# Expert weights of a two-layer hybrid encoder: two experts of a pair in one transfer, and the last down matrix in tiles

## The chip, the cores and the metric

The kernel runs on one core of a Trainium2 chip. The metric is the device time of one execution in microseconds, the median of three runs. A profiled execution of its own gives the trace; durations below come from that one.

## The reference, cut to what matters

Two layers (DEPTH 2), 256 tokens of width 1024, all in float32. A layer is a mixer (an mLSTM branch and an attention branch, merged, projected, added to x) and then a mixture of 32 experts. What the change touches is the second half:

```
t = rms_norm(x) * (1 + scale2) + shift2               # 256 x 1024
combine[256, 32] = weights of the top 2 experts of the top group, else 0
for 32 experts e:
    act = silu(t @ w_gate[e]) * (t @ w_up[e]) * combine[:, e]     # 1024 x 512 twice
    out += act @ w_down[e]                                        # 512 x 1024
x = x + gate2 * out
```

Each expert has three matrices of 2 MB, so a layer reads 192 MB of expert weights, once each. (MB and KB of tiles are binary here; the GB/s and MB of profile rows are decimal.)

## The kernel before, in words

**Places for weights.** A weight tile is 1 MB: 128 partitions times `SLOT` = 2048 floats (8 KB per partition). Tiles stand in numbered slots: 16 of one large buffer, the arena (`at`, L96), three of a region "y" and four of a region "x" (`region`, L83), one spare in the mixer. The mixer uses most of the arena for its own data and streams its weights through four arena slots (`BASE`: 0, 1, 2, 15), the three y slots and a few that are lent for a time. In the experts 18 slots take weights: 13 of the arena, three y, two x. They come free one after the other as the mixer ends: `release` at L1030 (8, 11, 12), in the order word `free:7:13:14` (L50), at L1073 (y and 6), at L1112 (x) and at L1400 (4 and 5).

**The order of transfers.** The whole list of weight tiles is written out beforehand (`plan`, L123, filled at L249 to L288): per pair of experts gate, up and down, each in two halves `h` of the contraction, each half as one tile of expert 2i and one of expert 2i+1, so 12 tiles a pair. `pump` (L162) takes the next entry, picks the first free slot that `fits` (L138) allows, and issues one transfer from SP's queue (L176); if no slot is free, the list waits. `done` (L185) gives a slot back after its last matmul and pumps again. All of this is decided when the program is built; on the chip SP runs the transfers in that order, each waiting for the readers of its slot.

**The experts.** 16 pairs (L1417). At most 64 rows of an expert are gathered (CAP), so the two experts of a pair share PE side by side, each in 64 of its 128 columns. `gate_up` (L1264) takes for each half both experts' tiles and interleaves their matmuls; then `act_mul`, `act_T`, and `down` (L1287), `leave`, `scatter`. Every other pair gathers rows for two pairs. After pair 11 (`MIDDLE`) comes `rest` (L1384): a conditional block for experts with more than 64 rows, with SP transfers of its own into tile `y` (L1367, L1377). The down matrix of the last pair is read by `down_last` (L1327) in two halves of 512 output columns; its transfers (L277 to L282) cut the columns out of a tile of 1024, so that each is 512 KB in pieces of 2 KB.

**Between layers.** The plan goes on with the next layer's first modulation tiles ("ada", `EARLY`), which `fits` lets into BASE, y, and arena slots 11 and 13 (L146), and with the mixer's weights.

**Queues.** Weights go by SP's queue alone. ACT's and POOL's queues carry a few small loads. PE and SP follow the program's order (`MANUAL`, L59).

Of the kernel before, what the change touches and what calls it, by code (L numbers as in the profile page):

```python
# [18 lines left out]
P = 128  # L19
# [4 lines left out]
DEPTH = 2  # L24
# [15 lines left out]
ONCE = (8, 9, 10, 11)  # L40
MIDDLE = 11
BF16 = mybir.dt.bfloat16
EARLY = (4, 5)
FIRST = (0, 2, 1, 3)
PREP = 60
# [14 lines left out]


def trunk(ctx, tc, x, c, b_ada, b_in, mlstm_norm_g, norm2_g, final_g,
          rope, gate_t, up_t, down_t, ada_t, in_t, branch_t, out_t, packs, router, out, dbg=None, depth=DEPTH):
    nc = tc.nc
    V, A, G, T = nc.vector, nc.scalar, nc.gpsimd, nc.tensor
    dbg = dbg or {}
# [12 lines left out]

    pools = {}  # L80
    tiles = {}

    def region(kind, name, types, side=None):  # L83

        if kind in pools:
            assert not any(r[1][0] == kind for r in ring.values())
            pools.pop(kind).close()
        es = ExitStack()
        pool = es.enter_context(tc.tile_pool(name=name, bufs=1, reuse_waits="tile", side=side))
        tiles[kind] = [pool.tile([P, SLOT], dt, name=f"{name}{i}") for i, dt in enumerate(types)]  # L90
        pools[kind] = es

    def wide(t, off, a):
# [2 lines left out]
    def at(slot, off, *shape):  # L96
        n = 1
        for s in shape:
            n *= s
        a = arena[:, slot * SLOT + off:slot * SLOT + off + n]  # L100
# [37 lines left out]
    def fits(slot, key):  # L138
        kind, s = slot
        if kind == "z":  # L140
            return key[0] not in ("wg", "wu", "wd", "fin")
        late = key[0] in ("wg", "wu", "wd", "wm", "wa", "wo")
        if (late and st["phase"] > 4 * key[1]) or slot in usual or (slot in opened and st["phase"] % 4 < 2):
            return True
        if key[0] == "ada" and kind == "a" and key[2] in ((EARLY, range(4))[key[1] == 0]):
            return s in (ONCE if key[1] == 0 else (11, 13))  # L146
        return False

    def release(slots):
# [12 lines left out]
    def pump():  # L162
        while st["sent"] < len(plan):
            key, src, shape, phase = plan[st["sent"]]
            if phase > st["phase"]:
                return
            if shape is None:
                src()
            else:
# [79 lines left out]
    for l in range(depth):  # L249
        if l == 0:  # L250
            for b in FIRST:
                plan_ada(0, b)
        else:
            plan_ada(l, EARLY[0])
        for it in stream(l):
            if it[0] in DENSE:
                sh = (8, 256) if it[0] == "akv" else (4, 512)
                add((it[0], l, *it[1:]), in_t[l, W_IN.index(it)].rearrange("p (k c) -> p k c", k=sh[0]), sh)
            elif it[0] == "r":
                plan_ada(l, it[1])  # L260
            else:
                plan_ada(l + 1, it[1])
            if l and it == ("q", 0, 0):
                plan_ada(l, EARLY[1])
            if it == ("k", 0, 0):
                add(("late", l), lambda l=l: late_loads(l), None, 4 * l)
            if it == ("k", 0, 1):
                add(("late2", l), lambda l=l: late_loads2(l), None, 4 * l)
        for j in range(2):
            for i, nm in enumerate(("wm", "wa")):  # L270
                add((nm, l, j), branch_t[l, i, j].rearrange("p (k c) -> p k c", k=4), (4, 512))
        for j in range(2):
# [26 lines left out]
    maskt = cst.tile([P, 3, P], F32, name="maskt")  # L299
    iot = cst.tile([P, P], F32, name="iot")  # L300
    desc = cst.tile([P, 8], F32, name="desc")
    fold = cst.tile([P, 32], F32, name="fold")
    fold2 = cst.tile([P, 64], F32, name="fold2")
    xs = cst.tile([P, NT, D], F32, name="xs")
# [12 lines left out]
    def setup():  # L317
# [140 lines left out]


    def mixer(l, p):  # L460
        region("x", f"R{l}", [F32R] * 4)
# [449 lines left out]

        def branch():
            if not yy:
                region("y", f"Y{l}", [F32R] * 3, "right")
# [157 lines left out]
        region("y", f"B{l}", [F32] * 3, "right")  # L1072
# [27 lines left out]
        region("x", f"X{l}", [F32] * 2 + [F32R] * 2)  # L1100
        return pL, lc, ssn, xa, sh2c


    def experts(l, p, pL, lc, ssn, xa, sh2c):
# [222 lines left out]
        def down_last(i, owT):  # L1327

            for n in range(2):
                pd = ps.tile([P, 512], F32, tag="f", name=f"pd{n}")  # L1330
                for h in range(2):
                    w = [wt("wd", l, 2 * i + e, n, h) for e in range(2)]
                    for kk in range(2):
                        for e in range(2):
                            T.matmul(pd[CAP * e:CAP * e + CAP, :], lhsT=aT[:, 2 * h + kk, CAP * e:CAP * e + CAP],  # L1335
                                     rhs=w[e][:, kk, :], start=h == 0 and kk == 0, stop=h == 1 and kk == 1,
                                     tile_position=(0, CAP * e))
                    for e in range(2):
                        done("wd", l, 2 * i + e, n, h)
# [7 lines left out]
                turn_rows(range(2, 4))  # L1347


        def rest_block(e, base):  # L1350
# [12 lines left out]
            for w in (gate_t, up_t):  # L1363
                pg = ps.tile([P, 512], F32, tag="f", name="pgr")
                for h in range(4):
                    wc = y.rearrange("p (a b) -> p a b", a=2)
                    nc.sync.dma_start(wc, w[l, ds(e, 1), h // 2].rearrange("o p (k f) -> p (o k) f", k=4)  # L1367
                                      [:, 2 * (h % 2):2 * (h % 2) + 2])
# [5 lines left out]
            act_T()  # L1374
            pd = [ps.tile([P, 512], F32, tag="f", name="pdr0"), ps.tile([P, 512], F32, tag="f", name="pdr1")]
            for k in range(4):
                nc.sync.dma_start(y, down_t[l, ds(e, 1), k // 2].rearrange("o p (k f) -> p (o k) f", k=2)[:, k % 2])  # L1377
# [6 lines left out]
        def rest():  # L1384
            full = nc.values_load(ci[0:1, NE:NE + 1], min_val=0, max_val=S,
                                  skip_runtime_bounds_check_because="a count of at most 256 rows")
            with tc.If(full > CAP):
                with tc.For_i(0, NE, 1) as e:
                    ne = nc.values_load(ci[0:1, ds(e, 1)], min_val=0, max_val=S,
                                        skip_runtime_bounds_check_because="a count of at most 256 rows")  # L1390
                    with tc.If(ne > CAP):
                        for base in (CAP, CAP + P):
                            rest_block(e, base)

        nextp = None
        oh = onehot(0)
# [61 lines left out]
    region("y", "B", [F32] * 3, "right")  # L1458
    with tc.manual_schedule(engines=MANUAL):
        p = setup()  # L1460
        for l in range(depth):
# [33 lines left out]
def laid_out(inputs):  # L1495
# [22 lines left out]
    def every(a):  # L1518
# [14 lines left out]
    return {**experts, "ada_t": whole(ada, (L, 12, 2, P, SLOT)), "in_t": whole(np.stack(tiles, 1), (L, len(W_IN), P, SLOT)),  # L1533
            "branch_t": whole(branch, (L, 2, 2, P, SLOT)), "out_t": whole(wo, (L, 2, 2, P, SLOT)),
            "packs": whole(packs, (L, P, NPK)), "router": whole(router, (L, P, 288))}

# [25 lines left out]
```

## Time and profile before

| | |
|---|---|
| median of 3 runs | 1473.15 us (1472.9 to 1474.9) |
| the profiled execution | 1472.51 us, of which the span (first to last instruction) is 1470.4 us |
| PE busy | 1336.9 us (91%); TensorE's granted clock 0.974 on average |
| DVE, ACT, POOL busy | 42%, 27%, 18% of the span |
| DMA | 521.31 MB in 77542 packets, 355 GB/s on average |
| weight tiles | SP's queue, 86.5% of 16 DMA engines' time over the span |

The page gives the busy time of each engine, and the span in 40 slices of 36.8 us. A busy PE is not a PE at its peak, since the ends of matmuls are modelled. A packet is one piece that one of the 16 DMA engines moves; the packets under 512 B are the marks of 4 bytes with which an engine reports its part of a transfer.

### The profile page before, as it was taken

Reading aid. Unit: us, or ns where it says so; the run is one execution under the profiler, and the core shown is the slowest. Engines: PE = TensorE matmul, PEld = TensorE weight load, DVE = VectorE, ACT = ScalarE, POOL = GpSimd, SP = SyncE. Lnnn points to the kernel's source line nnn. Section 1 sums busy time; section 2 is a strip of 40 time slices with the busy share of each in tenths; the row PEclk is TensorE's granted clock in tenths of the full one; section 3 lists DMA queues with packets and bytes.
Section 4 is the critical chain, followed back from the end, with each engine's and each line's share of the span. In section 5 each row is a group of like instructions: output and inputs, shape, how many; then the busy total and the mean of one; then the engine's idle time right before and its main releaser. Section 6 shows DMA issues by size and latency. Waiting matters only on the chain. (4 is left out here: it accounts for less than half of the span.)

```text
span 1470.4 us, 20138 instructions
## 1 busy us (share of the span) xinstructions
PE 1336.9 (91%) x7836; PEld 777.5 (53%) x7837; DVE 617.7 (42%) x1376; ACT 403.3 (27%) x755; POOL 263.5 (18%) x295
## 2 busy tenths in 40 slices
PE   6899998799999989889889999998999999987996
PEld 3778788734443434334359788883443443433432
DVE  3786755613323213213268777553332232223223
ACT  3636563311111101001056366541110110101101
POOL 2543336200000000000035533550000000000000
PEclk8999999899999999999999999998999999999998
DMA  9966697589999999999996645667999999999996
GB/s 383 368 257 238 253 366 276 205 367 419 419 420 419 420 420 419 420 393 399 413 411 258 241 175 233 233 261 294 420 419 419 420 419 419 420 419 418 372 420 236
DMA packets 77542, 521.31 MB, mean 355 GB/s; under 512 B 9472, under 2 KB 9472, under 8 KB 16256
## 3 DMA queue, kind: packets, MB, share of 16 engines
q1 hardware_dynamic: 75968, 515.95, 86.5%
q0 software_dynamic: 608, 2.14, 0.4%
q10 hardware_dynamic: 864, 1.85, 0.3%
q8 instruction: 65, 1.06, 0.3%
q14 instruction: 37, 0.30, 0.1%
HBM read 518.86 MB, written 1.05 MB: 354 GB/s over the span
## 5 line engine op out<-in xcount | busy, mean ns | idle before, releaser
L1270 PE MATMUL pgu<-arena 128*64 128x512 f32 x1504 | 376.0, 595 | 21.1 <-DMA arena<-in_up_t_dram 13.0
L1270 PEld LDWEIGHTS pgu<-arena 128*64 128x64 f32 x1504 | 121.6, 137 | 246.7 <-issue 193.7
L1279 DVE SCALAR_TENSOR_TENSOR arena<-pgu,wsl,arena 128x512 f32<-128x512 f32 x32 | 24.0, 751 | 389.4 <-PE pgu L1270 389.4
L1294 PE MATMUL pd<-arena 128*64 128x512 f32 x680 | 160.3, 594 | 7.3 <-ACT arena L1285 7.3
L1226 POOL TENSOR_TENSOR arena<-oh,arena 128x256 f32<-128x256 f32 x32 | 19.6, 617 | 737.6 <-DVE oh L1220 471.1
L549 PE MATMUL pd<-R,R 128*128 128x256 f32 x1056 | 137.7, 289 | 3.3 <-DVE arena L589 1.7
L471 POOL TENSOR_TENSOR R<-arena,R 128x512 fp32r<-128x512 f32 (+1 forms) x74 | 112.9, 1528 | 147.4 <-ACT R L490 113.2
L549 PEld LDWEIGHTS pd<-R,R 128*128 128x128 f32 x1056 | 131.4, 195 | 10.7 <-issue 6.7
L530 PE MATMUL pd<-R,R 128*128 128x256 f32 x1008 | 132.1, 289 | 4.7 <-ACT R L490 3.6
L530 PEld LDWEIGHTS pd<-R,R 128*128 128x128 f32 x1008 | 125.3, 194 | 14.2 <-issue 5.7
L1305 DVE TENSOR_TENSOR y<-pd,arena 128x512 f32<-128x512 f32 x64 | 44.1, 691 | 199.6 <-PE pd L1294 167.7
L1270 PE MATMUL pgu<-B,arena 128*64 128x512 f32 x384 | 116.2, 594 | 4.1 <-DMA B<-in_up_t_dram 2.7
L1306 ACT CAST yh<-y 128x512 fp32r<-128x512 f32 x64 | 39.5, 618 | 237.2 <-DVE y L1305 237.2
L1294 PEld LDWEIGHTS pd<-arena 128*64 128x64 f32 x680 | 50.2, 137 | 95.3 <-issue 85.6
L471 DVE TENSOR_TENSOR R<-arena,R 128x512 fp32r<-128x512 f32 (+1 forms) x82 | 73.8, 909 | 55.8 <-ACT R L490 49.3
L1242 PE MATMUL pG<-oh,X 128*128 128x256 f32 x512 | 73.9, 307 | 16.0 <-DVE oh L1220 15.7
L1317 DVE TENSOR_TENSOR xs<-xs,psc 128x512 f32<-128x512 f32 x128 | 79.4, 681 | 18.2 <-PE psc L1314 18.2
L1242 PEld LDWEIGHTS pG<-oh,X 128*128 128x128 f32 x512 | 70.1, 213 | 27.3 <-issue 26.4
L490 ACT CAST R<-arena 128x1024 fp32r<-128x1024 f32 x66 | 68.8, 1043 | 51.9 <-PE pd L549 25.9
L1285 ACT COPY arena<-pat 128x512 f32<-128x512 f32 x32 | 18.8, 586 | 216.3 <-PE pat L1284 216.3
L1246 ACT ACTIVATE arena<-pG,sh2c 128x256 f32<-128x256 f32 x64 | 30.4, 475 | 156.1 <-DVE arena L1248 156.1
L1278 ACT ACTIVATE arena<-pgu 128x512 f32<-128x512 f32 x32 | 19.1, 597 | 189.7 <-PE pgu L1270 189.7
(323 smaller groups left out, 1680.1 us busy)
## 6 DMA issues: line engine op xcount, KB each, us to landing
arena<-in_up_t_dram SPq DMA_DIRECT2D x110, 1024.0 KB, 19.9
arena<-in_down_t_dram SPq DMA_DIRECT2D x85, 1024.0 KB, 19.9
arena<-in_gate_t_dram SPq DMA_DIRECT2D x78, 1024.0 KB, 19.9
arena<-in_ada_t_dram SPq DMA_DIRECT2D x31, 1024.0 KB, 6.4
B<-in_gate_t_dram SPq DMA_DIRECT2D x30, 1024.0 KB, 19.9
arena<-in_in_t_dram SPq DMA_DIRECT2D x23, 1024.0 KB, 6.8
X<-in_gate_t_dram SPq DMA_DIRECT2D x20, 1024.0 KB, 19.9
X<-in_down_t_dram SPq DMA_DIRECT2D x20, 1024.0 KB, 19.9
```

Of the source, the lines that this page charges most:

```text
L471: eng.tensor_tensor(dst, full, hi.bitcast(F32), op=ALU.subtract)
L490: A.copy(wh, w)
L530: T.matmul(acc[key][o][:, 0:S], lhsT=w[:, kk, P * o:P * o + P], rhs=x_[:, 4 * kh + kk], start=kh == 0 and i == 0 and kk == 0, stop=kh == 1 ...
L549: T.matmul(acc[key][t][:, 0:256], lhsT=x_[:, 4 * kh + kk, P * t:P * t + P], rhs=w[:, kk], start=kh == 0 and i == 0 and kk == 0, stop=kh == ...
L1242: T.matmul(pG[:, kk, 0:n], lhsT=x_[:, t, P * k:P * k + P], rhs=oh[:, t, :], start=i == 0, stop=i == 3)
L1246: A.activation(xg[k][:, 0:n], pG[:, kk, 0:n], AF.Identity, bias=sh2c[:, k:k + 1])
L1270: T.matmul(pg[CAP * e:CAP * e + CAP, :], lhsT=xg[4 * h + kk][:, P * (i % 2) + CAP * e:P * (i % 2) + CAP * e + CAP], rhs=w[e][:, kk, :], st ...
L1279: V.scalar_tensor_tensor(ac.rearrange("p k q -> p (k q)"), pu, wsl[:, 0:1], sl, op0=ALU.mult, op1=ALU.mult)
L1294: T.matmul(pd[n][CAP * e:CAP * e + CAP, :], lhsT=aT[:, 2 * h + kk, CAP * e:CAP * e + CAP], rhs=w[e][:, kk, 512 * n:512 * n + 512], start=h ...
L1305: V.tensor_tensor(y[:, cs], pd, gt2b[:, cs], op=ALU.mult)
L1306: A.copy(yh[:, cs], y[:, cs])
L1317: V.tensor_tensor(xx, xx, pq, op=ALU.add)
```

## The change: what it does

The host lays the expert weights out per pair: for each pair, matrix and half, partition p holds the 8 KB of expert 2i and then the 8 KB of expert 2i+1, 16 KB in a row. `pump` looks for two free slots that lie side by side (`TWINS`) and fills both with one transfer of 2 MB. For that the arena's slots are put in another order in memory (`LAID`, `WHERE`), and the slots 0 and 1 of y and of x are one tile of double width each. There are nine such twins, which are the same 18 slots; the ninth is arena slot 4 and y slot 2, which lie apart and take two transfers of 1 MB. The last pair's down matrix is laid out in four tiles of 1 MB ("tail"), one per half of the output columns and half of the contraction, both experts in one, 8 KB in a row per partition. `fits` lets the first early modulation block into slot 13 alone and the second into 11 alone. `rest_block` reads its matrices from the new layout, with a small table `whose` (two iotas in the setup) to find pair and place.

```diff
+LAID = (0, 1, 2, 15, 7, 8, 11, 12, 13, 14, 5, 6, 4, 3, 9, 10)
+WHERE = {s: i for i, s in enumerate(LAID)}
+TWINS = tuple((("a", LAID[i]), ("a", LAID[i + 1])) for i in range(0, 12, 2)) + (
+    (("y", 0), ("y", 1)), (("x", 0), ("x", 1)), (("a", 4), ("y", 2)))
...
-        tiles[kind] = [pool.tile([P, SLOT], dt, name=f"{name}{i}") for i, dt in enumerate(types)]
+        for i, (dt, n) in enumerate(types):
+            t = pool.tile([P, n * SLOT], dt, name=f"{name}{i}")
+            tiles[kind] += [t[:, k * SLOT:(k + 1) * SLOT] for k in range(n)]
...
-            return s in (ONCE if key[1] == 0 else (11, 13))
+            return s in (ONCE if key[1] == 0 else (13,) if key[2] == EARLY[0] else (11,))
...
+            elif key[0] in ("wg", "wu", "wd") and len(key) == 4:
+                nm, l, i, h = key
+                ok = [t for t in TWINS if all(s in free and fits(s, key) for s in t)]
+                if not ok:
+                    return
+                two = min(ok, key=lambda t: max(free.index(s) for s in t))
...
+                if other[0] != kind:
+                    for e in range(2):
+                        nc.sync.dma_start(place(two[e], (1, SLOT))[:, 0], src[:, SLOT * e:SLOT * e + SLOT])
+                elif kind == "a":
+                    o = WHERE[s] * SLOT
+                    nc.sync.dma_start(arena[:, o:o + 2 * SLOT], src)
+                else:
+                    nc.sync.dma_start(whole[kind, s], src)
+                for e in range(2):
+                    ring[nm, l, 2 * i + e, h] = (place(two[e], shape), two[e])
...
-                            for e in (2 * i, 2 * i + 1):
-                                add((nm, l, e, q, h), w[l, e, h].rearrange("p (k f) -> p k f", k=2)
-                                    [:, :, 512 * q:512 * q + 512], (2, 512))
+                            add(("tail", l, q, h), tail_t[l, q, h].rearrange("p (k f) -> p k f", k=4), (4, 512))
...
-                    for e in (2 * i, 2 * i + 1):
-                        add((nm, l, e, h), w[l, e, h].rearrange("p (k f) -> p k f", k=sh[0]), sh)
+                    add((nm, l, i, h), w[l, i, h], sh)
...
+        G.iota(whose[:, 0:NE], pattern=[[1, NPAIR], [0, 2]], base=0, channel_multiplier=0)
+        G.iota(whose[:, NE:2 * NE], pattern=[[0, NPAIR], [1, 2]], base=0, channel_multiplier=0)
...
-    experts = {nm: whole(g[w].reshape(L, NE, 2, n, P, SLOT // n).transpose(0, 1, 2, 4, 3, 5), (L, NE, 2, P, SLOT))
+    experts = {nm: whole(g[w].reshape(L, NPAIR, 2, 2, n, P, SLOT // n).transpose(0, 1, 3, 5, 2, 4, 6),
+                         (L, NPAIR, 2, P, 2 * SLOT))
```

## Rows read from the trace of the kernel before

**Rows 1.** The page: its first line, and the 40 slices of DMA (busy share of the DMA engines in tenths, and GB/s).
```profile
span 1470.4 us, 20138 instructions
DMA  9966697589999999999996645667999999999996
GB/s 383 368 257 238 253 366 276 205 367 419 419 420 419 420 420 419 420 393 399 413 411 258 241 175 233 233 261 294 420 419 419 420 419 419 420 419 418 372 420 236
```

**Rows 2.** Stretches of the span, in us from its start: length, busy time (and count) of PE, PE's weight loads, DVE, ACT, POOL, then TensorE's granted clock, the share of the DMA engines, GB/s. The first two lie inside the experts of layer 0 and layer 1 (ten pairs each), the next two are the stretches from the first transfer after the start of the experts to the last "up" tile.
```profile
330.00:630.00 300.00, 274.21 (x1318) 116.09 (x1314) 85.65 (x148) 35.50 (x63) 4.93 (x8) 1.00 1.01 419
1020.00:1320.00 300.00, 281.44 (x1356) 117.56 (x1356) 81.28 (x141) 36.12 (x64) 5.55 (x9) 1.00 1.01 419
297.00:730.00 433.00, 400.47 (x1911) 168.57 (x1908) 115.60 (x201) 50.15 (x89) 8.97 (x19) 0.99 1.00 414
1009.00:1443.00 434.00, 402.38 (x1912) 167.61 (x1910) 115.62 (x201) 50.19 (x89) 8.59 (x14) 0.99 1.00 414
```

**Rows 3.** The waits of SP's queue over the whole span, the longest of them (line of SP, who ended the wait, us in total, times, longest), and the issues of the commonest tile (count, KB each, median us from issue to landing).
```profile
SPq L176 <- DMA arena<-in_up_t_dram: 167.2, 84, 3.3
SPq L176 <- DMA arena<-in_down_t_dram: 137.5, 68, 2.3
SPq L176 <- DMA arena<-in_gate_t_dram: 110.6, 52, 3.5
...
arena<-in_up_t_dram SPq DMA_DIRECT2D x110, 1024.0 KB, 19.9
```

**Rows 4.** DMA packets from 330 to 630 us (300 us of tiles with 8 KB per partition), and SP's queue in that stretch: packets, MB, the time of the packets as a share of 16 engines.
```profile
DMA packets 17258, 125.78 MB, mean 419 GB/s; under 512 B 1916, under 2 KB 1916, under 8 KB 1916
q1 hardware_dynamic: 17241, 125.55, 101.0%
```

**Rows 5.** The same from 1444 to 1452 us, while the last down matrix of layer 1 comes in pieces of 2 KB.
```profile
DMA packets 1556, 3.11 MB, mean 389 GB/s; under 512 B 96, under 2 KB 96, under 8 KB 1556
q1 hardware_dynamic: 1556, 3.11, 104.9%
```

**Rows 6.** The same from 41.6 to 45.4 us, three loads of a row of 4 KB that every partition gets (L242).
```profile
DMA packets 319, 1.62 MB, mean 426 GB/s; under 512 B 33, under 2 KB 33, under 8 KB 210
```

**Rows 7.** SP's transfers in order of time where the experts of layer 0 and of layer 1 begin: start, us, line, tile, count; four short stretches of each, and the DMA's stretch between the last fill of a slot and the first refill.
```profile
268.49 3.71 SPq L176 DMA_DIRECT2D arena<-in_gate_t_dram  x2
277.18 0.80 SPq L176 DMA_DIRECT2D X<-in_gate_t_dram  x2
278.68 0.33 SPq L176 DMA_DIRECT2D arena<-in_up_t_dram  x1
288.76 0.33 SPq L176 DMA_DIRECT2D arena<-in_up_t_dram  x1
297.14 0.80 SPq L176 DMA_DIRECT2D arena<-in_up_t_dram  x2
...
979.17 3.71 SPq L176 DMA_DIRECT2D arena<-in_gate_t_dram  x2
987.86 0.80 SPq L176 DMA_DIRECT2D X<-in_gate_t_dram  x2
989.36 0.33 SPq L176 DMA_DIRECT2D arena<-in_up_t_dram  x1
999.45 0.33 SPq L176 DMA_DIRECT2D arena<-in_up_t_dram  x1
1009.02 0.81 SPq L176 DMA_DIRECT2D arena<-in_up_t_dram  x2
...
293.00:299.00 6.00, 6.00 (x31) 2.25 (x31) 1.72 (x5) 2.23 (x3) 1.19 (x2) 1.00 0.17 22
```

**Rows 8.** The conditional block after pair 11: SP's instructions of its line (count, ns, first and last start in the span), who waited for it, and the DMA where it stops in layer 0.
```profile
L1387 SPq EVENT_SEMAPHORE  x18: 17/17/17, 648.2 to 1373.8; - x18
L1387 SPq COMPARE_BRANCH  x2: 50/50/50, 642.8 to 1354.3; - x2
  DVE y L1305: 19.5, 2
658.00:664.00 6.00, 6.00 (x30) 2.01 (x28) 2.00 (x4) 1.23 (x2) 0.00 (x0) 1.00 0.36 142
```

**Rows 9.** The chain of waits that ended last, its last part: start, us, what.
```profile
1412.64 19.88 DMA arena<-in_gate_t_dram
1438.25 7.97 PE pgu L1270 x32
1447.87 0.59 ACT arena L1285
1448.51 3.68 PE pd L1335 x16
1454.38 0.96 PE psc L1314 x3
1455.35 1.89 PE pd L1335 x8
1465.21 0.71 ACT arena L1471
```

**Rows 10.** PE in order of time at the change of layers: start, us, line, operation, tiles, and in brackets its idle time and what ended it.
```profile
748.68 0.33 PE L457 MATMUL pxt<-ident,xs 128*128 128x128 f32 x1 [0.32 <-DVE xs L1317]
750.19 1.92 PE L385 MATMUL pada<-arena,condp 128*32 128x512 f32 x16
```

**Rows 11.** POOL in order of time in the setup: its last iota, and its next instruction.
```profile
4.21 0.14 POOL L350 IOTA desc<- 128x8 f32 x1
26.24 0.73 POOL L471 TENSOR_TENSOR R<-arena,R 128x256 fp32r<-128x256 f32 x1 [21.89 <-ACT arena L673]
```

More of the change, by code (lines that the diff above doesn't have):

```diff
@@ L62, in trunk @@
 def trunk(ctx, tc, x, c, b_ada, b_in, mlstm_norm_g, norm2_g, final_g,
-          rope, gate_t, up_t, down_t, ada_t, in_t, branch_t, out_t, packs, router, out, dbg=None, depth=DEPTH):
+          rope, gate_t, up_t, down_t, tail_t, ada_t, in_t, branch_t, out_t, packs, router, out, dbg=None, depth=DEPTH):
     nc = tc.nc
@@ L81, in trunk @@
     tiles = {}
+    whole = {}
     def region(kind, name, types, side=None):
@@ L89, in region @@
         pool = es.enter_context(tc.tile_pool(name=name, bufs=1, reuse_waits="tile", side=side))
-        tiles[kind] = [pool.tile([P, SLOT], dt, name=f"{name}{i}") for i, dt in enumerate(types)]
+        tiles[kind] = []
+        for i, (dt, n) in enumerate(types):
+            t = pool.tile([P, n * SLOT], dt, name=f"{name}{i}")
+            tiles[kind] += [t[:, k * SLOT:(k + 1) * SLOT] for k in range(n)]
+            whole[kind, len(tiles[kind]) - n] = t
         pools[kind] = es
@@ L99, in at @@
             n *= s
-        a = arena[:, slot * SLOT + off:slot * SLOT + off + n]
+        o = WHERE[slot] * SLOT + off
+        a = arena[:, o:o + n]
         if len(shape) > 1:
@@ L140, in fits @@
         if kind == "z":
-            return key[0] not in ("wg", "wu", "wd", "fin")
-        late = key[0] in ("wg", "wu", "wd", "wm", "wa", "wo")
+            return key[0] not in ("wg", "wu", "wd", "tail", "fin")
+        late = key[0] in ("wg", "wu", "wd", "tail", "wm", "wa", "wo")
         if (late and st["phase"] > 4 * key[1]) or slot in usual or (slot in opened and st["phase"] % 4 < 2):
@@ L168, in pump @@
                 src()
+            elif key[0] in ("wg", "wu", "wd") and len(key) == 4:
[4 more added lines that the diff above has]
+                two = min(ok, key=lambda t: max(free.index(s) for s in t))
+                for s in two:
+                    free.remove(s)
+                (kind, s), other = two
+                if other[0] != kind:
[8 more added lines that the diff above has]
+                    ring[nm, l, 2 * i + e, h] = (place(two[e], shape), two[e])
             else:
@@ L301, in trunk @@
     desc = cst.tile([P, 8], F32, name="desc")
+    whose = cst.tile([P, 2 * NE], I32, name="whose")
     fold = cst.tile([P, 32], F32, name="fold")
@@ L460, in mixer @@
     def mixer(l, p):
-        region("x", f"R{l}", [F32R] * 4)
+        region("x", f"R{l}", [(F32R, 1)] * 4)
         es = ExitStack()
@@ L913, in branch @@
             if not yy:
-                region("y", f"Y{l}", [F32R] * 3, "right")
+                region("y", f"Y{l}", [(F32R, 1)] * 3, "right")
                 yy[:] = [wide(t, 0, 8) for t in tiles["y"][0:2]]
@@ L1071, in mixer @@
         assert not any(r[0] is retired[0] for r in ready)
-        region("y", f"B{l}", [F32] * 3, "right")
+        region("y", f"B{l}", [(F32, 2), (F32, 1)], "right")
         release([("y", s) for s in range(3)] + [("a", 6)])
@@ L1099, in mixer @@
         es.close()
-        region("x", f"X{l}", [F32] * 2 + [F32R] * 2)
+        region("x", f"X{l}", [(F32, 2), (F32R, 1), (F32R, 1)])
         return pL, lc, ssn, xa, sh2c
@@ L1331, in down_last @@
                 for h in range(2):
-                    w = [wt("wd", l, 2 * i + e, n, h) for e in range(2)]
+                    w = wt("tail", l, n, h)
                     for kk in range(2):
@@ L1335, in down_last @@
                             T.matmul(pd[CAP * e:CAP * e + CAP, :], lhsT=aT[:, 2 * h + kk, CAP * e:CAP * e + CAP],
-                                     rhs=w[e][:, kk, :], start=h == 0 and kk == 0, stop=h == 1 and kk == 1,
+                                     rhs=w[:, 2 * e + kk, :], start=h == 0 and kk == 0, stop=h == 1 and kk == 1,
                                      tile_position=(0, CAP * e))
-                    for e in range(2):
-                        done("wd", l, 2 * i + e, n, h)
+                    done("tail", l, n, h)
                     if (n, h) == (1, 0):
@@ L1347, in down_last, with rest_block @@
                 turn_rows(range(2, 4))
-        def rest_block(e, base):
+        def rest_block(e, at_, base):
             pe = small("pe", NT, 1)
@@ L1366, in rest_block @@
                     wc = y.rearrange("p (a b) -> p a b", a=2)
[L1367 to L1368 removed]
+                    nc.sync.dma_start(wc, w[l, ds(at_[0], 1), h // 2].rearrange("o p (e k f) -> (o p) e k f", e=2, k=4)
+                                      [:, ds(at_[1], 1), 2 * (h % 2):2 * (h % 2) + 2].rearrange("p e k f -> p (e k) f"))
                     for kk in range(2):
@@ L1376, in rest_block @@
             for k in range(4):
-                nc.sync.dma_start(y, down_t[l, ds(e, 1), k // 2].rearrange("o p (k f) -> p (o k) f", k=2)[:, k % 2])
+                nc.sync.dma_start(y, down_t[l, ds(at_[0], 1), k // 2].rearrange("o p (e k f) -> (o p) e k f", e=2, k=2)
+                                  [:, ds(at_[1], 1), k % 2].rearrange("p e f -> p (e f)"))
                 for n in range(2):
@@ L1391, in rest @@
                     with tc.If(ne > CAP):
+                        at_ = [nc.values_load(whose[0:1, ds(NE * v + e, 1)], min_val=0, max_val=(NPAIR - 1, 1)[v],
+                                              skip_runtime_bounds_check_because="a constant table") for v in range(2)]
                         for base in (CAP, CAP + P):
-                            rest_block(e, base)
+                            rest_block(e, at_, base)
         nextp = None
@@ L1456, in experts @@
         return nextp
-    region("y", "B", [F32] * 3, "right")
+    region("y", "B", [(F32, 2), (F32, 1)], "right")
     with tc.manual_schedule(engines=MANUAL):
@@ L1530, in laid_out @@
     router = r.reshape(L, KD, P, 36).transpose(0, 2, 1, 3)
-    experts = {nm: whole(g[w].reshape(L, NE, 2, n, P, SLOT // n).transpose(0, 1, 2, 4, 3, 5), (L, NE, 2, P, SLOT))
+    experts = {nm: whole(g[w].reshape(L, NPAIR, 2, 2, n, P, SLOT // n).transpose(0, 1, 3, 5, 2, 4, 6),
+                         (L, NPAIR, 2, P, 2 * SLOT))
                for nm, w, n in (("gate_t", "w_gate", 4), ("up_t", "w_up", 4), ("down_t", "w_down", 2))}
-    return {**experts, "ada_t": whole(ada, (L, 12, 2, P, SLOT)), "in_t": whole(np.stack(tiles, 1), (L, len(W_IN), P, SLOT)),
+    tail = g["w_down"][:, NE - 2:].reshape(L, 2, 2, 2, P, 2, 512).transpose(0, 5, 2, 4, 1, 3, 6)
+    return {**experts, "tail_t": whole(tail, (L, 2, 2, P, SLOT)), "ada_t": whole(ada, (L, 12, 2, P, SLOT)), "in_t": whole(np.stack(tiles, 1), (L, len(W_IN), P, SLOT)),
             "branch_t": whole(branch, (L, 2, 2, P, SLOT)), "out_t": whole(wo, (L, 2, 2, P, SLOT)),
```

## The prediction

> **What bounds the kernel now.** I read the slices of the page first. Counted from 0, slices 9 to 20 and 28 to 38 have the DMA engines 90% busy or more, mostly at about 420 GB/s; the others mostly do not [rows 1]. These are the experts of the two layers. So the next view was busy time by stretch: inside the experts the DMA share is 1.01 for 300 us on end at 419 GB/s, while PE is busy 274.2 us of 300, that is 27.4 us per pair against 30.0 us that a pair's 12 MB take [rows 2]. The DMA stream sets the pace, PE has 2.6 us of slack a pair. The whole stretches from the first refill to the last "up" tile run at 414 GB/s, nearly the same [rows 2]. The waits of SP's queue agree: it waits mostly for earlier transfers to land, and a tile lands 19.9 us after its issue [rows 3], which is eight times 2.5 us: eight transfers are in flight, and the DMA engines never lack work. Last the end: the chain that ended last runs through a gate tile that lands at 1412.64 + 19.88 = 1432.5 us; four "up" tiles of 2.5 us follow, so the last lands near 1442.5, and from there the chain is PE, DVE and ACT alone [rows 9]. What moves the end is thus the landing of the last "up" tile in each layer: most of a layer's 192 MB come at the stream's pace, and only a faster stream, or fewer holes in it, makes the kernel faster.
>
> **How many bytes count.** In both layers the 18 slots are full before the experts' first matmuls give any back: the last fill is issued at 288.76 and 999.45, the refill starts at 297.14 and 1009.02, and between them the DMA is 0.17 busy [rows 7]. Of a layer's 192 MB, 18 are in by then and 4 are the last down matrix, so 170 MB, or 85 transfers of 2 MB, lie on the path, per layer.
>
> **The price of a packet.** The change halves the number of packets: a 2 MB pair now is, per DMA engine, 16 packets of 8 KB and 2 marks; it becomes 8 of 16 KB and 1 mark, 9 packets fewer for the same bytes. No row shows a weight packet of 16 KB, so I fit engine time = A per packet + B per byte to two rows of the same queue. From 330 to 630: 16 x 300,000 ns = 17258 A + 125.78e6 B [rows 4]. In the pieces of 2 KB: 16 x 8,000 ns = 1556 A + 3.11e6 B [rows 5]. That gives A = 8.25 ns and B = 0.0370 ns per byte. A 2 MB pair now costs 18 x 8.25 + 131072 x 0.0370 = 5002 ns; with 9 packets less, 4928 ns. The saving of 74 ns (1.5%) times 85 is 6.3 us per layer, **12.6 us** for both.
>
> Bounds. If I take the packets' own records instead of the clock (104.9% and 101.0% of 16 engines, which overlap), A comes out at 12.6 ns and the saving at 2 x 85 x 9 x 12.6 = 19.2 us [rows 4, 5]. From below, three loads with pieces of 4 KB ran at 426 GB/s [rows 6], faster than 8 KB; a fit to them gives A = -10.6 ns, no saving but 16.2 us more. But those read one row of 4 KB for all partitions, while the 2 KB row reads weights, each byte once, from the same queue; it is the nearer one, and I take 8.25. The ends kept are -19.2 and +16.2.
>
> **The other parts.**
> - Twins. A free slot now waits for its neighbour. Cover: the idle DMA before the refill. In the worst case four pairs and the split one come last. From 268.49 and 979.17, when the slots of the last projection come free, 10 MB at 4.93 us per 2 MB would need 24.6 us: done at 293 and 1004; the last pair by itself, not before 288.76 + 4.9 = 294 and 999.45 + 4.9 = 1004; the refill is at 297.14 and 1009.02 [rows 7]. So 0. Once that cover is used up, each pair that is later costs 4.9 us.
> - Granularity. PE takes both experts' tiles of a half before its matmuls interleave, and gives them back together; it waits for the same bytes in the same order. 0.
> - SP issues some 90 transfers fewer a layer. It mostly waited for landings [rows 3]; eight transfers in flight are now 16 of the 18 slots, so SP will wait for PE's release instead, with only later transfers behind it. 0.
> - The conditional block. SP stands at its branch at 642.8 because its transfers were late, then waits until all have landed; the DMA has a hole at 658 to 664 (share 0.36, 3.8 us lost), and DVE's y waits 19.5 us in two times [rows 8]. SP will reach the branch earlier, but the same 18 tiles must land before it goes on. The block stays, so no gain, and PE then has 18 MB in hand, so no loss. 0.
> - The last down matrix. 4.19 MB at 419 instead of 389 GB/s is 0.8 us sooner [rows 4, 5]. At the end PE asks for it from 1448.51, six us after the last "up", and for its last part at 1455.35, and no DMA stands in the chain [rows 9]: 0. At the change of layers PE goes from the turned rows at 748.68 to the modulation at 750.19 without waiting for a transfer [rows 10]: 0, at best -0.8. With the two slots for modulation narrowed to one each, at worst a tile of 2.5 us comes late, with eight transfers in flight ahead of it: 0.
> - Two iotas of about 0.14 us in the setup, where POOL then idles 21.9 us [rows 11]: 0.
> - What is late next: PE. A pair would take 6 x 4.93 = 29.6 us of DMA against PE's 27.4, so PE gives the stream's whole gain through, and would cap it only at 9%.
>
> Sum: 1472.51 - 12.6 = 1459.9 for an execution like the profiled one; that one lay 0.64 below the median, so **1460.5 us** against 1473.15.
>
> **Rivals.**
> - Half the price (chance 0.20). The 2 KB pieces are cut out of rows of 4 KB in memory, so part of A may be the price of cut rows and not of packets. With A = 4.1 the gain is 6.3 us: 1466.9. For it: the 4 KB row, which sees no price at all [rows 6]. Against: that row reads the same bytes over and over. The Trainium skill (DMA: Bandwidth & Descriptors, Bandwidth, on why small descriptors are slow) has a fixed 3 cycles per packet and 32 bytes of descriptor; at its 850 MHz that is, as an estimate, 4.7 ns a packet, which would be 7.2 us and 1466; the trace's fit is higher.
> - No price (chance 0.11). The stream may stand at a limit of bytes, not of packets: 2 KB and 8 KB pieces differ by only 7%, and 420 GB/s is never passed for long [rows 1]. Then the time stays at 1473. A gain eaten up by twins that come one pair too late in each layer ends here too.
> - Slower (chance 0.09). A larger piece per partition moves more slowly per byte, as the 4 KB row against the 8 KB rows would have it [rows 4, 6]: neighbouring partitions' rows then lie 16 KB apart instead of 8 KB, in the stream of the experts, on all 170 pairs. The price by that fit is 95 ns a pair, 16.2 us: 1489.3. It decides as soon as a 16 KB packet takes longer than two of 8 KB and a half mark. Against it: from 2 KB to 8 KB the rate rises. The Trainium skill (DMA: Bandwidth & Descriptors, Latency and other measured facts) has a rule in this direction: rows at large powers of two apart lose rate, 207 against 214 GB/s at 512 KiB; at 16 KB it gives no figure, and no run here shows it.
>
> **How the numbers follow.** The forecast, a gain of 9 to 19 us, has 0.60; half the price 0.20; no price 0.11; slower 0.09. The bound of 0.2% is 2.9 us, about what a measurement of this kernel can tell from no change. So faster 0.80, same 0.11, slower 0.09. The range reaches from the upper end of the saving (1473.15 - 19.2 = 1454, and the 0.8 of the change of layers) to below no price: 1453.5 to 1470, which leaves out the last two cases.
>
> **What would show it.** Right: half as many packets for the same bytes, packets of 16 KB, the expert stretches at 425 to 426 GB/s, the refill still at 297 and 1009, the last gate and "up" tiles 6 us earlier in layer 0 and 12 to 13 in layer 1, the same 28 us from the last "up" to the end. SP's waits turn from landings to PE. Wrong: packets that stay at 8 KB; the rate at 419 or below; DMA shares under 1 after 299 or before the refill, with SP waiting for a slot while another is free; PE busy near 100% of a pair; a mixer of layer 1 that is longer.

## The result, and the profile after

The changed kernel takes 1457.95 us (median of 6 runs, 1457.42 to 1460.13) against 1473.03 us for the kernel before in the same session (6 runs, 1471.09 to 1474.9): ratio 0.9900, 95% interval 0.9887 to 0.9913, or 15.1 us less. The forecast was 1460.5 us in a range of 1453.5 to 1470. The profiled execution took 1458.14 us, its span is 1456.4 us.

The page of the kernel after, its first line and the slices of DMA (tenths busy, GB/s):

```profile
span 1456.4 us, 19790 instructions
DMA  9866594899999999999996556459999999999995
GB/s 385 350 267 251 234 366 170 329 387 424 426 427 424 425 428 425 425 384 416 424 415 239 227 188 241 178 232 370 426 425 424 428 425 425 427 425 424 373 427 231
```

Most slices that had 419 or 420 in [rows 1] now have 424 to 428: the expert stretches run faster as a whole. Stretches of the kernel after (length, busy time and count of PE, PE's weight loads, DVE, ACT, POOL, granted clock, DMA share, GB/s), the first two as in [rows 2], the others from just after the first refill to just before the last "up" tile has landed:

```profile
330.00:630.00 300.00, 275.04 (x1339) 118.61 (x1339) 87.24 (x152) 36.93 (x66) 6.11 (x10) 0.98 1.01 425
1020.00:1320.00 300.00, 282.44 (x1373) 117.45 (x1368) 83.70 (x145) 36.20 (x65) 4.92 (x8) 0.99 1.01 426
297.00:722.00 425.00, 392.74 (x1898) 163.42 (x1894) 115.64 (x201) 50.17 (x89) 8.84 (x18) 0.99 1.00 421
1003.00:1428.00 425.00, 392.99 (x1898) 163.80 (x1894) 115.58 (x201) 50.17 (x89) 8.57 (x14) 0.99 1.00 421
```

DMA is still the bound (share 1.01) and PE still has slack. The same 300 us by packets, to be read against [rows 4]:

```profile
DMA packets 9778, 127.64 MB, mean 425 GB/s; under 512 B 1088, under 2 KB 1088, under 8 KB 1088
q1 hardware_dynamic: 9759, 127.39, 100.4%
```

17258 packets have become 9778, with 1.5% more bytes. They are more than half, since the split twin keeps its pieces of 8 KB. SP's transfers at the start of the experts (start, us, line, tile, count) show it, with the refills in two later stretches:

```profile
274.40 0.33 SPq L196 DMA_DIRECT2D X<-in_gate_t_dram  x1
275.92 0.33 SPq L191 DMA_DIRECT2D arena<-in_gate_t_dram  x1
276.30 0.42 SPq L191 DMA_DIRECT2D B<-in_gate_t_dram  x1
...
294.78 0.33 SPq L194 DMA_DIRECT2D arena<-in_up_t_dram  x1
...
1000.75 0.33 SPq L194 DMA_DIRECT2D arena<-in_up_t_dram  x1
```

Line 191 fills the ninth twin by two transfers; that occurs ten times a layer, once before the refill and nine times on the path. The refill begins at 294.78 and 1000.75, where [rows 7] had 297.14 and 1009.02. SP's waits before transfers of expert weights (who ended them, us in all, times, longest):

```profile
SPq L194 <- PE pd L1324: 108.6, 26, 10.5
SPq L194 <- PE pgu L1300: 107.6, 37, 8.8
...
SPq L194 <- DMA arena<-in_down_t_dram: 61.4, 17, 4.5
```

In [rows 3] the landings of earlier transfers were the longest waits of this kind; now it is PE giving slots back. (Over the whole span the longest single total belongs to the mixer in both kernels, a wait for DVE's `R`: 204.1 us before, which [rows 3] leaves out, and 148.4 after.) The chain that ended last (start, us, what):

```profile
1394.13 34.34 DMA B<-in_up_t_dram
1428.52 3.68 PE pgu L1300 x16
...
1434.48 3.68 PE pd L1365 x16
...
1441.33 1.89 PE pd L1365 x8
...
1451.20 0.70 ACT arena L1503
```

The last "up" tile lands at 1394.13 + 34.34 = 1428.5; from there it is engines alone, as in [rows 9], and 27.9 us to the end of the span.

**The span in five pieces.** For every kernel below I read two times per layer from its trace: the issue of the first refill (the first expert transfer once all slots have been filled), and the landing of the last "up" tile; the end of the span closes the account. "First refill" is that of layer 0, in us from the start of the span. "Stream" is from refill to last "up" of a layer, "between" from the last "up" of layer 0 to the refill of layer 1, "tail" from the last "up" to the end. All in us, one profiled execution each.

| kernel | first refill | stream 0 | between | stream 1 | tail | span |
|---|---|---|---|---|---|---|
| before | 297.14 | 433.30 | 278.58 | 433.50 | 27.89 | 1470.4 |
| after | 294.78 | 427.75 | 278.22 | 427.73 | 27.90 | 1456.4 |
| e1_2mb_8k | 294.18 | 433.59 | 275.60 | 433.89 | 27.90 | 1465.2 |
| e2_2mb_4k | 296.23 | 445.10 | 277.39 | 445.25 | 28.02 | 1492.0 |
| e3_two_1mb | 301.60 | 433.35 | 278.44 | 433.49 | 27.89 | 1474.8 |
| e4_pitch32 | 294.72 | 426.57 | 276.41 | 427.11 | 27.91 | 1452.7 |
| e5_after_hold | 298.29 | 427.36 | 275.57 | 428.31 | 28.39 | 1457.9 |
| e6_before_hold | 295.17 | 433.44 | 276.47 | 433.61 | 27.90 | 1466.6 |
| e7_tail_cut | 294.32 | 427.46 | 278.35 | 427.73 | 28.54 | 1456.4 |
| e8_eight_twins | 298.37 | 431.58 | 278.49 | 431.82 | 28.18 | 1468.4 |
| c1_after | 295.76 | 427.52 | 278.27 | 427.81 | 27.91 | 1457.3 |
| c2_pitch_hold | 295.33 | 426.56 | 276.44 | 427.04 | 27.89 | 1453.3 |
| c3_hold_again | 293.75 | 427.77 | 278.26 | 427.88 | 27.90 | 1455.6 |

Before to after, the streams give 5.55 + 5.77 = 11.3 us, the first refill 2.4, the rest 0.3: 14.0 of span. Among kernels with the same pieces and slots the streams repeat to some tenths of a microsecond (0.6 at most); the first refill and "between" do not, and they hold what a single execution scatters.

### The profile page after: what moved, and what is told of

It reads as the page before. It is cut to its first block, busy times and chain, and to the rows that moved or that the text cites. A ratio compares the mean times of both kernels' runs of the same rounds, so it can differ in the third digit from the quotient of the medians.

```text
span 1456.4 us, 19790 instructions
## 1 busy us (share of the span) xinstructions
PE 1324.0 (91%) x7836; PEld 771.7 (53%) x7837; DVE 615.3 (42%) x1376; ACT 403.4 (28%) x755; POOL 264.5 (18%) x297
## 5 line engine op out<-in xcount | busy, mean ns | idle before, releaser
L1300 PE MATMUL pgu<-arena 128*64 128x512 f32 x1376 | 325.9, 599 | 19.7 <-DMA arena<-in_gate_t_dram 12.6
L1300 PEld LDWEIGHTS pgu<-arena 128*64 128x64 f32 x1376 | 104.4, 138 | 232.1 <-issue 196.5
L1324 PE MATMUL pd<-arena 128*64 128x512 f32 x800 | 195.5, 595 | 21.8 <-ACT arena L1315 21.8
L1324 PEld LDWEIGHTS pd<-arena 128*64 128x64 f32 x800 | 60.0, 137 | 137.5 <-issue 107.9
L1300 PE MATMUL pgu<-B,arena 128*64 128x512 f32 x352 | 97.5, 594 | 2.3 <-DMA B<-in_up_t_dram 1.7
L1300 PE MATMUL pgu<-X,arena 128*64 128x512 f32 x320 | 72.3, 593 | 4.5 <-DMA X<-in_up_t_dram 4.5
```

The costliest lines, as they stand in the source:

```text
L1300: T.matmul(pg[CAP * e:CAP * e + CAP, :], lhsT=xg[4 * h + kk][:, P * (i % 2) + CAP * e:P * (i % 2) + CAP * e + CAP], rhs=w[e][:, kk, :], st ...
L1324: T.matmul(pd[n][CAP * e:CAP * e + CAP, :], lhsT=aT[:, 2 * h + kk, CAP * e:CAP * e + CAP], rhs=w[e][:, kk, 512 * n:512 * n + 512], start=h ...
```

## The experiments

Theories: (P) the streams are shorter because there are fewer packets for the same bytes; (Q) because transfers of 2 MB keep more bytes in flight and need fewer marks; (D) rows that lie further apart cost something. Later ones ask what the split twin and the tail are worth, and where the 2.4 us before the first refill come from. Ratios are to the kernel before, with 95% intervals.

**e1_2mb_8k: 2 MB transfers, but pieces of 8 KB.** The experts of a pair follow one another in memory and not within a row:

```diff
+PIECES = 2
-                    add((nm, l, i, h), w[l, i, h], sh)
+                    add((nm, l, i, h), w[l, i, h].rearrange("c p f -> p c f"), sh)
-                    nc.sync.dma_start(arena[:, o:o + 2 * SLOT], src)
+                    nc.sync.dma_start(arena[:, o:o + 2 * SLOT].rearrange("p (c f) -> p c f", c=PIECES), src)
```

> The changed kernel, but the two experts of a pair lie in memory one after the other, so that a transfer is still 2 MB into a twin, in pieces of 8 KB. Packet theory (the gain of the stream is 8.25 ns for each packet that is not there): 17 packets per engine and pair instead of 9, so 66 ns on each of some 76 whole pairs of a layer, +10.0 us, about 1468; the experts at 420 GB/s. Rival, depth of the queue (eight transfers in flight are 16 MB instead of 8 MB, and that makes the stream faster): still about 1458 and 425 GB/s.

Measured: 1468.35 us (6 runs), 0.9967 (0.9956 to 0.9979). Its packets from 330 to 630 us:

```profile
DMA packets 16432, 125.88 MB, mean 420 GB/s; under 512 B 1077, under 2 KB 1077, under 8 KB 1077
```

The marks are down to after's number, the packets are back, and the streams are as long as before's (433.59 and 433.89). So the transfers of 2 MB give nothing in the streams. The time is the 1468 that P expected. The 5 us or so by which the kernel still beats the kernel before (4.9 by the ratio) lie outside of the streams in the traces: "first refill" (3.0) and "between" (3.0, which scatters).

**e2_2mb_4k: the same with pieces of 4 KB** (`PIECES = 4`).

> The same with pieces of 4 KB, still 2 MB in one transfer (the split twin too has pieces of 4 KB). Packet theory: 33 packets instead of 9, 198 ns on each of 152 pairs, and 132 ns on 18 split ones, +32 us, about 1490, the experts at 409 GB/s. Rival, that pieces of 4 KB cost nothing (what the three loads of a 4 KB row before the change said): 1458. Depth of the queue: 1458.

Measured: 1493.82 us (4 runs), 1.0136 (1.0121 to 1.0150).

```profile
DMA packets 30957, 122.68 MB, mean 409 GB/s; under 512 B 1041, under 2 KB 1041, under 8 KB 30943
q1 hardware_dynamic: 30943, 122.48, 102.3%
```

The streams are 11.5 and 11.4 us longer than e1's, for 85 pairs with 16 packets more on each of the 16 engines: 11.4 us / (85 x 16) = 8.4 ns a packet. So the 16 added packets cost, each, about what the fit had (8.25). The time lies 3.8 us above the expected 1490.

**e3_two_1mb: the twins filled by two transfers of 1 MB** (pieces of 8 KB, 2 marks):

```diff
-                    nc.sync.dma_start(arena[:, o:o + 2 * SLOT], src)
+                    for e in range(2):
+                        nc.sync.dma_start(arena[:, o + SLOT * e:o + SLOT * e + SLOT], src[:, SLOT * e:SLOT * e + SLOT])
```

> The changed kernel, its layout and its twins, but each twin filled by two transfers of 1 MB in pieces of 8 KB. Packet theory: 18 packets instead of 9, 74 ns on 152 pairs, +11.3 us, about 1469, and 1 us above the kernel with one transfer of 2 MB in pieces of 8 KB. Depth of the queue: also 1469, but 11 us above that kernel. The two theories part at the difference of the two kernels.

Measured: 1472.54 us (12 runs), 0.9993 (0.9984 to 1.0003).

```profile
DMA packets 17274, 125.85 MB, mean 420 GB/s; under 512 B 1922, under 2 KB 1922, under 8 KB 1922
```

Beside e1 there are 845 marks more for the same bytes: a mark has no price that can be seen. (The size of the transfers changes with the number of marks; strictly, it is the two together that cost nothing.) The streams (433.35 and 433.49) are e1's and before's. By time it lies 4.2 us above e1, which neither P (1 us) nor Q (11 us) had; this is outside of the streams, and e6 explains 3 us of it.

**e4_pitch32: rows 32 KB apart.** The two halves of a matrix lie next to each other in memory, so that the 16 KB of neighbouring partitions are 32 KB apart:

```diff
-                    add((nm, l, i, h), w[l, i, h], sh)
+                    add((nm, l, i, h), w[l, i, :, h], sh)
```

> The changed kernel, with the two halves of a matrix next to each other in memory, so that the rows of 16 KB of a transfer lie 32 KB apart instead of 16 KB. Packet theory: nothing changes, 1458. Rival, distance of rows (larger powers of two lose rate): slower, and then a part of the gain of 16 KB pieces was lost to the distance in the change too.

Measured: 1456.26 us (4 runs), 0.9889 (0.9874 to 0.9904).

```profile
DMA packets 9779, 127.66 MB, mean 426 GB/s; under 512 B 1088, under 2 KB 1088, under 8 KB 1088
```

Twice the distance costs nothing: D is out for distances of 16 and 32 KB. The streams are even 1.2 and 0.6 us shorter. A packet is also one unbroken run in memory, here and in e1 and e2; no run tells the price of a packet from that of a shorter run.

**e7_tail_cut: the change with the last down matrix as before**, eight transfers of 512 KB in pieces of 2 KB:

```diff
-                            add(("tail", l, q, h), tail_t[l, q, h].rearrange("p (k f) -> p k f", k=4), (4, 512))
+                            for e in range(2):
+                                add(("tail", l, e, q, h), w[l, i, h].rearrange("p (e k f) -> p e k f", e=2, k=2)
+                                    [:, e, :, 512 * q:512 * q + 512], (2, 512))
```

> The changed kernel with the last down matrix as before: eight transfers of 512 KB in pieces of 2 KB. The prediction's step has it hidden at both ends: 1458, at most +0.8. Rival, it is on the path at the change of layers (four more slots taken, the next layer's first tiles later): +2 us or more.

Measured: 1458.28 us (5 runs), 0.9886 (0.9869 to 0.9903). The last pieces of down, from 1428.5 to 1436 us, are slow ones again:

```profile
DMA packets 1501, 2.90 MB, mean 387 GB/s; under 512 B 87, under 2 KB 87, under 8 KB 1501
```

The span is the same 1456.4 us, the tail 28.54 instead of 27.90: the layout of the tail is worth 0.6 us at most, and e5, which leaves the tail alone, has 28.39.

**e8_eight_twins: no split twin**, so 16 slots and no pair in pieces of 8 KB:

```diff
-    (("y", 0), ("y", 1)), (("x", 0), ("x", 1)), (("a", 4), ("y", 2)))
+    (("y", 0), ("y", 1)), (("x", 0), ("x", 1)))
```

> The changed kernel without the ninth, split twin: pairs go into eight twins (16 MB), all in transfers of 2 MB. Theory that the bytes which are not in before the refill lie on the path: 2 MB more in each layer, 2 x 4.9 us, less 18 split pairs that become whole, 18 x 74 ns: +8.5 us, about 1466.5. Rival, the number of slots filled before the start doesn't matter (DMA has slack there, or PE sets the pace at the start): 1457 to 1458.

Measured: 1467.86 us (6 runs), 0.9949 (0.9934 to 0.9965). The streams are 3.8 and 4.1 us longer than after's. That is one pair more on the path (4.9 us), less nine pairs that have lost eight packets each (9 x 74 ns = 0.7 us): 4.2. The expected 1466.5 was missed by 1.4 us. So the count of bytes that the path carries is right, and the ninth twin pays although its pieces are small. (From 330 to 630 us the rate is 427 GB/s.)

**e6_before_hold: the kernel before, with one wait moved.** The view for this is PE in order of time just ahead of the experts of layer 0, where the refill comes sooner. A stretch of 50 matmuls (the views also count two or three that reach into it), one kernel per fence: the kernel before, in the columns of [rows 2],

```profile
251.60:262.90 11.30, 7.58 (x52) 6.98 (x50) 3.96 (x11) 3.53 (x8) 4.15 (x5) 0.85 0.78 325
```

and the kernel after:

```profile
252.20:260.20 8.00, 6.28 (x53) 5.84 (x51) 4.39 (x11) 3.53 (x8) 4.27 (x5) 1.00 0.62 229
```

The same work takes 11.3 us before and 8.0 after: PE idles 3.7 instead of 1.7 us, and is busy 1.3 us longer, with a granted clock of 0.85 in the mean of the stretch (a part of it at 1.2 GHz) against 1.00 after. What PE waits for, in the kernel before (start, us, line, operation, count, and in brackets the idle time and what ended it),

```profile
257.12 1.38 PE L1058 MATMUL pxa<-ident,arena 128*128 128x128 f32 x4 [3.71 <-POOL arena L1049]
```

and after:

```profile
255.52 0.44 PE L1088 MATMUL pxa<-ident,arena 128*128 128x128 f32 x2 [1.47 <-POOL arena L1079]
```

POOL (GpSimd) waits for rows that DVE (VectorE) makes. Ahead of these rows in DVE's order stands the sum `c1`, modulation columns that need the next layer's parameters (`pk`), a small load from POOL's queue. DVE's wait for it, before:

```profile
DVE c1b L696 <- DMA pk<-in_packs_dram: 5.5, 1, 5.5
```

and after (in order of time, with what follows on DVE):

```profile
252.14 0.60 DVE L726 TENSOR_TENSOR c1b<-c,pk 128x16 f32<-128x16 f32 x1 [2.93 <-DMA pk<-in_packs_dram]
252.78 0.17 DVE L695 SCALAR_TENSOR_TENSOR A<-c1b,pk 128x8 f32<-128x8 f32 x1
252.86 0.75 DVE L1076 TENSOR_TENSOR arena<-pd,arena 128x256 f32<-128x256 f32 x2
```

The load is issued at 247.7 before and at 248.3 after. SP's queue in those microseconds, before:

```profile
243.03 0.80 SPq L176 DMA_DIRECT2D B<-in_up_t_dram  x2
243.88 1.56 SPq L176 DMA_DIRECT2D B<-in_down_t_dram  x1
245.54 10.67 SPq L176 DMA_DIRECT2D arena<-in_down_t_dram  x3
```

and after:

```profile
243.67 0.33 SPq L196 DMA_DIRECT2D B<-in_up_t_dram  x1
254.28 0.33 SPq L194 DMA_DIRECT2D arena<-in_up_t_dram  x1
```

Before, SP issues six tiles of 1 MB between 243 and 256 us; after, one pair of 2 MB, and the next only once both slots of a twin are free. The small load's time to landing is the first number here (its other transfer, in the setup, is the last), before:

```profile
DMA to landing us min/median/max: 6.5/10.5/14.6
```

and after:

```profile
DMA to landing us min/median/max: 3.8/9.2/14.6
```

To test it, the edit takes the sum `c1` out of the way of DVE's rows and leaves all transfers as they are:

```diff
+        first["lo"] = marks["lo"]
         release([("a", 4), ("a", 5)])
...
-            V.tensor_tensor(c1, mods[l], cols[:, 80:96], op=ALU.add)
+            with tc.issue_after(first["lo"].ins):
+                V.tensor_tensor(c1, mods[l], cols[:, 80:96], op=ALU.add)
```

> The kernel before with the same instruction held back. Theory of the wait: DVE's 5.5 us at 254 us go, the refill starts 3.5 to 4 us earlier, about 1469. With both kernels so, their difference should be the stream's alone, 11 to 12.6 us. Rival: 1473.

Measured: 1470.14 us (12 runs), 0.9971 (0.9958 to 0.9984), that is 4.3 us less (2.4 to 6.2). The stretch of 50 matmuls:

```profile
253.60:260.60 7.00, 6.22 (x52) 5.78 (x51) 3.43 (x7) 3.53 (x8) 4.22 (x5) 1.00 1.02 424
```

The DMA is as busy as before (424 GB/s, and the load still takes 6.4 us), but nobody waits: 11.3 us have become 7.0, the same 4.3 (2.9 of idle PE, 1.4 of PE busy for longer). In the profiled execution the first refill came 2.0 us sooner, not the expected 3.5 to 4, since the stretch itself began 2 us later. In e3 each half of a twin goes out as soon as its own slot is free; one more tile of 1 MB is in flight when the load is issued, the load takes 6.3 us, and the wait is there again:

```profile
256.40:267.40 11.00, 7.58 (x52) 6.98 (x51) 4.00 (x11) 3.53 (x8) 4.20 (x5) 0.84 0.39 144
```

11.0 us here against 8.0 in e1 are 3 of the 4.2 us between them; in e1, with the same pieces in whole transfers of 2 MB, the load takes 4.0:

```profile
251.90:259.90 8.00, 6.28 (x52) 5.84 (x51) 4.32 (x11) 3.54 (x8) 4.26 (x5) 1.00 0.60 224
```

The low clock does not belong to the long wait alone. In e8 the load takes 3.6 us and PE idles 1.7 us, as in the kernel after, and yet a part of the stretch ran at 1.2 GHz:

```profile
254.00:263.50 9.50, 7.77 (x53) 7.34 (x51) 4.40 (x11) 3.53 (x8) 4.37 (x5) 0.82 0.60 221
```

So 2.0 of the 3.3 us between before and after are the shorter wait. The other 1.3, the clock, stood in both traces with the long wait (before and e3), but also in e8, one of the seven with the short one; whether it belongs to the wait is open.

**e5_after_hold: the same edit in the changed kernel.**

> The changed kernel with one DVE instruction held back: the modulation columns of layer 1 (c1), which DVE's queue has at 252 us and which waits there for the load of the next layer's small parameters, come after the experts' start instead. Theory of the wait (in the change the refill started 2.4 us earlier because that load met fewer weight transfers and DVE waited 2.9 us instead of 5.5 us): the rest of that wait goes, down to the projection's matmuls that end near 251: -1.5 us, about 1456.5. Rival, the 2.4 us are chance of a run or PE's clock: 1458.

Measured: 1457.68 us (4 runs), 0.9882 (0.9866 to 0.9897). The wait is gone and the 50 matmuls take 7.1 us instead of 8.0, but this execution's first refill is late for another reason (its mean clock in the first 95 us was 0.89, against 0.95 in after's), and the time can't be told from after's: the expected 1456.5 is not shown. Against e6, in the same session, it is 12.5 us less, where 11 to 12.6 was expected for the streams alone; the streams of these two traces differ by 11.4.

**c1_after, c2_pitch_hold, c3_hold_again: the changed kernel, both small edits, and the hold alone, on one chip.**

> The changed kernel once more, unedited, beside the two below on one chip. All theories: 0.990 of the kernel before (0.989 to 0.991), so the differences of under 2 us between it and its variants can be read against a measured spread.

> The changed kernel with both small edits: the halves next to each other in memory (rows 32 KB apart) and VectorE's wait for the next layer's parameters moved behind its work on the rows for the first experts. If both edits gave what their single runs suggest (about -1 us each), it lies 2 us below the changed kernel, near 1456; if those were the spread of runs, within 1 us of it.

> The changed kernel with VectorE's wait for the next layer's parameters moved alone, a second time. A real gain of about 1 us, as the time of TensorE's matmuls at the start of the experts has it (7.1 against 8.0 us for the same 50): 1 us below the changed kernel. If the wait is hidden in the changed kernel: level with it.

Measured: 1459.0 us, 0.9904 (0.9885 to 0.9922); 1456.28 us, 0.9889 (0.9872 to 0.9905); 1456.72 us, 0.9889 (0.9872 to 0.9905), 4 runs each. The stretch of 50 matmuls in c3:

```profile
251.90:259.00 7.10, 6.32 (x53) 5.88 (x51) 3.54 (x7) 3.53 (x8) 4.33 (x5) 1.00 0.72 261
```

The traces repeat (hold: 7.1 instead of 8.0 us; rows 32 KB apart: streams of 426.56 and 427.04, as in e4). The medians lie 2.7 (both edits) and 2.3 us (hold) below c1's, but the intervals overlap. The version with both edits is level with e4 alone (1456.26); that either beats the changed kernel is likely from the traces and not shown by the times.

## Why the prediction was right, and where it was not

- **The bound: right.** DMA's rate moved from 419 to 425 and 426 GB/s, as forecast (425 to 426), and each layer's last "up" moved with it: 7.9 us sooner in layer 0 and 14.0 in layer 1 (forecast 6, and 12 to 13).
- **The price of a packet: right in sum, with two errors that cancel.** Forecast: 74 ns a pair, as 9 packets of 8.25 ns. Measured: (5.55 + 5.77) / 2 / 76 = 74 ns a pair. But the mark was priced like a packet of weights, and it costs nothing that can be seen (e3 against e1), so eight packets carry it: 9.3 ns each (a mark belongs to eight packets, so the rival's "half mark" is an eighth); from e1 to after it is (5.84 + 6.16) / 2 / (76 x 8) = 9.9 ns, and from 4 to 8 KB 8.4 ns. The trace speaks against the estimate of 4.7 ns from the Trainium skill (DMA: Bandwidth & Descriptors, Bandwidth): the price is about twice as high here.
- **The count: mis-sized.** 85 pairs a layer were priced, but the split twin keeps 8 KB pieces, and nine of the 85 go through it. The term should have been 76 x 74 ns = 5.6 us a layer, 11.2 in all; the streams gave 11.3. The diff said so (two transfers of 1 MB), and the sum overlooked it.
- **"The refill still at 297 and 1009": wrong, 294.78 and 1000.75.** The 1009 contradicts the forecast itself, in which a stream shorter by 6.3 us in layer 0 moves layer 1's refill to 1003. No cost of the twins showed between the last projection and the refill, as forecast; but a gain of theirs was put at nothing without being looked for. It lay 40 us earlier: a transfer that now waits for a second slot leaves SP's queue emptier just when POOL's small load comes, DVE waits 2.9 instead of 5.5 us for it, and the 50 matmuls there take 3.3 us less, 2.0 of them less idle time and 1.3 the clock. The wait is shown as a cost by e6 (4.3 us by time and by trace); that the emptier queue shortens the load's landing (6.5 to 3.8 us) rests on a comparison of traces: 6.3 to 6.5 us in before, e3 and e6, where three or four tiles of 1 MB were in flight when it was issued, 3.6 to 4.1 in the other ten, with one pair of 2 MB in flight. The nearest to a test is e1 against e3 (4.0 and 6.3 us): the same pieces, cut into transfers differently. No experiment was made to vary only the queue.
- **Tail, granularity, SP's issues: 0, right** (e7; e1 and e3).
- **The conditional block: 0, right.** The hole stays; in the kernel after it lies some 8 us sooner, as far as the first refill and the faster stream have moved it (2.4 and about 5):

```profile
650.00:656.00 6.00, 6.00 (x30) 2.01 (x28) 1.59 (x3) 0.95 (x2) 0.00 (x0) 1.00 0.51 172
```

  [rows 8] has 0.36 at 658 to 664; PE is busy through both.
- **The rivals.** Half the price (6.3 us) and no price are excluded by the streams' 11.3 us. The slower one wanted a loss from rows that lie further apart; at 16 KB the rate rose, at 32 KB (e4) it did not fall. The Trainium skill's rule on it (DMA: Bandwidth & Descriptors, Latency and other measured facts) has figures for rows from 512 KiB apart; no run here has such a distance.
- **The sum.** Forecast 12.6 us; measured 15.1. Streams 11.3 and the 50 matmuls' 3.3 are 14.6. The remaining 0.5 is less than what executions of one kernel differ by. The two traces differ by 14.0, since after's stretch of 50 began 0.6 us later. That the forecast came within 2.5 us is in part luck: its term for the packets was 1.3 us too large, and one of 2 to 3 us was missing.

**What stays open.** "Between" takes 275.6 to 278.6 us with nearly the same program there. It goes roughly with the clock granted in it: the time at 1.2 GHz between the last "up" of layer 0 and the refill of layer 1 is 17 us in e1 and e5 (275.6), 20 in e2, e4, e6 and c2 (276.4 to 277.4), 24 in after, c1 and c3 (278.2 to 278.3) and 27 in before, e3, e7 and e8 (278.3 to 278.6). A part of it lies early in the mixer. From 64.5 to 90.5 us after the last "up" of layer 0, the kernel after:

```profile
787.00:813.00 26.00, 21.53 (x134) 17.93 (x132) 23.18 (x85) 4.92 (x6) 9.53 (x12) 0.77 0.24 85
```

and e1:

```profile
792.00:818.00 26.00, 20.98 (x145) 17.41 (x144) 24.05 (x88) 5.51 (x7) 10.16 (x12) 0.87 0.31 106
```

A mean of 0.87 instead of 0.77 over 26 us is worth 2.6 us at most, as an estimate, and "between" is 275.60 there against 278.22. This stretch alone does not settle it: it has 0.80 in e4 and before alike, whose "between" is 276.41 and 278.58. PE is busy 21 of the 26 us in after and e1, so it has idle time just there; why the clock falls for longer in one execution was not tried. It is no property of one kernel: e5 (275.57) and c3 (278.26) are the same program.

## What to carry to other kernels

Where a stretch runs at a DMA share of 1, price a change of layout by the packets that each DMA engine is spared (here 8 to 10 ns per packet of weights; transfers of 1 and of 2 MB made no difference), and multiply by the transfers that really get the new shape: the odd buffer out keeps the old price. Then ask of every transfer that is held back or bundled not only what it delays, but which small load on another queue it lets through: a wait of 5 us for a load of parameters, in front of an engine's more urgent work, cost 4.3 us (2.4 to 6.2, e6), against 11.3 us for all the packets. Such a load's consumer belongs behind the work that doesn't need it.

## What the runs showed of the hardware

Two things I had not expected. The rate still rises from pieces of 8 KB to 16 KB (420 to 425 GB/s, e1 and after) at nearly the same price per packet as from 4 to 8 KB (409 to 420), while twice the bytes per transfer and half the marks do nothing. And rows 32 KB apart, with the two halves of a matrix next to each other, make the streams about 1 us a layer shorter (426.57 and 426.56 against 427.36 to 427.77 in the five executions with rows 16 KB apart and 18 slots, layer 0); the cause was not looked for.
